# A hybrid decoder layer on one core: router fed from rows without the first norm, output projection in another order

## The chip, the core and the metric

The kernel runs on one core of a Trainium2 chip. Its time is the device time of one execution in microseconds (us); three runs are summed up by their median, and one further execution is recorded by the profiler. TensorE does the matmuls (PE in the profile), VectorE is DVE, ScalarE is ACT, GpSimd is POOL, and SyncE is SP, whose queue issues nearly all weight loads.

## What is computed

One layer for 256 tokens of width 1024: a token mixer with an output projection, a norm, a mixture of 32 experts of which each token uses four, a second norm, and a small gated sublayer with a third norm. Cut to what bears on the change:

```
y = token_mixer(x, ...)                      # ends with (g_a*y_a + g_b*y_b + g_c*y_c) @ w_out
x = layer_norm(alpha * x + y, ln1_g, ln1_b)  # the first norm: (x - mean) * rstd * g + b
logits = x @ router_w + router_b             # 256 x 32
gates, experts = softmax and indices of the 4 largest
y = sum over a token's experts of gate * (swiglu(x @ w_gu[e] + b_gu[e]) @ w_down[e] + b_down[e])
x = layer_norm(alpha * x + y, ln2_g, ln2_b)
ple = sigmoid(x @ ple_w_gate) * (p @ ple_w_proj)
x = layer_norm(alpha * x + ple, ln3_g, ln3_b)
```

## The kernel before

**Stages.** The mixer ends at 440.17 us of the span, router and first gather at 457.04 us; then come the 32 experts, one by one, and the tail. The tokens are two tiles of 128 rows (t = 0, 1), the width is two halves of 512 columns (c) or eight blocks of 128 (k).

**Order in the mixer.** Work is written as strands (Python generators) that a small loop advances in turn, and as units: a unit is a list of products and an evacuation. Every engine runs its instructions in the order in which they were recorded. The output projection is one of these series of units: `both(kp)` is the first half of both tiles with two of the eight row blocks of `w_out`, `second(t, ...)` the second half of tile t. A weight block arrives by DMA and is split into a high and a low part (`HI`, `LO`, or the buffers `RV`, `KT`, `xh`, `xl`); three products use the two. `evac` adds the residual, takes the statistics, and starts `first_norm(t)` when a tile's two halves are done. `first_norm` writes the normalised rows to `xs`, transposes them (L1186) and multiplies them with the router's weights `rw` (L1192). `router` then finds the four largest of each row and the place of each token among the 64 slots of its experts (`posm`).

**Experts.** Tokens are gathered by a matmul: `oh` is a matrix of zeros and ones that the places give, `xs` times `oh` is the gathered, transposed activations (`gat`, L1448), which ACT copies to `xe` (L1449). A group is two experts (128 slots), so one gather of eight blocks in four pieces serves two experts. Two pieces fall into each expert of the group before, between the transposes and the down projection; their PSUM buffers are two (`ms`). The up projection (`gu`, L1485) and the down projection (`dn`, L1520) multiply with `w_gu` (8.39 MB an expert) and `w_down` (4.19 MB).

**Weights.** These 12.58 MB an expert come in tiles of 2 MiB through a ring of ten buffers: four (`F0` to `F3`) are filled with expert 0's `w_gu` during the mixer, and six (`w5` to `w0`) lie in memory that the mixer uses until its end. SP issues the loads in ring order: w5 and w4 (`w_down` of expert 0, L1387), w3 to w0 (`w_gu` of expert 1, L1375), F0 and F2 (`w_down` of expert 1), F1, F3, w5, w4 (`w_gu` of expert 2), and so on. Each issue waits until its buffer's last user is done, in order, so that one that waits holds all behind it. Issues also wait for earlier transfers with which they share one of eight completion semaphores (`DMAHW0` to `DMAHW7`), which ACT's loads use too. The two rows of the first norm, `ln1_g` and `ln1_b`, are loaded to all partitions (512 KB each) by ACT in the mixer, `norm_rows`.

**Result.** An expert's rows are spread back to the tokens by another matmul and added to `Y`; the first to be added also brings in alpha times the norm's rows (`fresh` in `spread`).

## Time and profile before

| what | us |
| --- | --- |
| median of 3 runs (lowest, highest) | 1422.58 (1421.93, 1425.25) |
| the profiled execution | 1420.59 |
| its span, first to last instruction | 1418.8 |
| PE busy in it | 1343.1 (95%) |
| DVE, ACT, POOL busy | 591.8, 372.4, 247.0 |

The page has in all 481.66 MB moved, 339 GB/s over the span. Over it, the granted clock of TensorE is 0.985 of full speed. PE's busy share is high in every stage, but an engine that is busy need not be the one that ends last: rows by stretch and the waits tell that.

### The profile page before, as it was taken

The page shows a single profiled execution, that of the slowest core. Times are in us where ns is not written, and L with a number is a line of the kernel's source. Part 1 is how long each engine was busy: PE and PEld are TensorE (multiplying, and loading weights), DVE is VectorE, ACT ScalarE, POOL GpSimd, SP SyncE. Part 2 cuts the span into 40 slices and gives each one's busy share as a digit, 9 for nine tenths or more (in the row PEclk, how much of TensorE's full clock was granted, in tenths as well). Part 3 has the DMA queues.
Part 4 walks back from the last instruction along what each step waited for, and adds up shares of the span by engine and source line. Part 5 has one row for each costly group of instructions (what it writes and reads, how often), then busy time and mean ns, then how long its engine had stood idle before and what let it go on. Part 6 is the DMA issues. An engine that isn't in the chain of part 4 may idle for free. (4 is left out here: it accounts for less than half of the span.)

```text
span 1418.8 us, 19330 instructions
## 1 busy us (share of the span) xinstructions
PE 1343.1 (95%) x7720; PEld 748.0 (53%) x7721; DVE 591.8 (42%) x1245; ACT 372.4 (26%) x743; POOL 247.0 (17%) x217
## 2 busy tenths in 40 slices
PE   8999989999999999999999999999999999989987
PEld 7989967888887334334333333333333333333326
DVE  6398985865565133223222222222223222222238
ACT  6767464644551111111111110111111100111122
POOL 5554864434561000000000000000000000000000
PEclk9999999999998999999999999999999999999998
DMA  9755455345888999999999999999999999999970
GB/s 264 215 137 138 133 180 168 113 135 181 307 303 339 367 427 430 428 428 426 428 429 428 428 426 429 430 428 428 426 429 430 428 427 428 429 428 428 428 296 30
DMA packets 122133, 481.66 MB, mean 339 GB/s; under 512 B 11340, under 2 KB 69340, under 8 KB 88632
## 3 DMA queue, kind: packets, MB, share of 16 engines
q1 hardware_dynamic: 120440, 477.16, 84.4%
q0 software_dynamic: 848, 1.86, 0.4%
q10 hardware_dynamic: 752, 1.38, 0.3%
q8 instruction: 62, 1.02, 0.3%
q14 instruction: 31, 0.25, 0.0%
HBM read 478.78 MB, written 3.42 MB: 340 GB/s over the span
## 5 line engine op out<-in xcount | busy, mean ns | idle before, releaser
L1485 PE MATMUL gu<-w,xe 128*64 128x512 f32 x1168 | 262.9, 598 | 6.6 <-DMA w<-in_w_gu_dram 6.6
L1485 PE MATMUL gu<-F,xe 128*64 128x512 f32 x880 | 199.2, 596 | 4.8 <-DMA F<-in_w_gu_dram 4.8
L428 POOL TENSOR_TENSOR LO<-w,HI 128x384 fp32r<-128x384 f32 (+1 forms) x113 | 168.4, 1491 | 165.9 <-ACT HI L423 154.6
L1485 PEld LDWEIGHTS gu<-w,xe 128*64 128x64 f32 x1168 | 81.7, 137 | 164.8 <-issue 144.1
L426 DVE TENSOR_TENSOR LO<-w,HI 128x640 fp32r<-128x640 f32 (+1 forms) x113 | 117.1, 1038 | 83.5 <-ACT HI L423 81.8
L1503 DVE TENSOR_SCALAR gc<-gu 128x256 f32<-128x256 f32 x64 | 26.9, 421 | 266.9 <-PE gu L1485 266.9
L1416 POOL DMA_DIRECT2D pt<-in_p_dram x1 | 0.8, 777 | 789.2 <-DVE lc L1507 789.2
L423 ACT CAST HI<-w 128x1024 fp32r<-128x1024 f32 x113 | 118.0, 1044 | 59.2 <-PE pjt L377 36.6
L1520 PE MATMUL dn<-w,hT 128*64 128x512 f32 x560 | 130.0, 607 | 2.0 <-ACT hT L1513 2.0
L1556 DVE TENSOR_TENSOR Y<-Y,cb 128x512 f32<-128x512 f32 x124 | 79.5, 682 | 116.3 <-PE cb L1545 116.3
L367 PE MATMUL pjt<-xh,HI 128*128 128x256 f32 x424 | 124.7, 294 | 0.0
L1485 PEld LDWEIGHTS gu<-F,xe 128*64 128x64 f32 x880 | 60.2, 136 | 119.0 <-issue 104.9
L367 PE MATMUL pjt<-xh,LO 128*128 128x256 f32 x424 | 120.5, 284 | 1.3 <-DVE LO L426 1.3
L367 PE MATMUL pjt<-xl,HI 128*128 128x256 f32 x424 | 120.1, 283 | 0.0
L1520 PE MATMUL dn<-F,hT 128*64 128x512 f32 x464 | 106.0, 598 | 0.0
L1504 ACT ACTIVATE sg<-gc 128x256 f32<-128x256 f32 x64 | 26.8, 419 | 286.4 <-DVE gc L1503 286.4
L1448 PE MATMUL gat<-oh,xs 128*128 128x128 f32 x512 | 76.2, 294 | 24.7 <-DVE oh L1456 19.9
L1448 PEld LDWEIGHTS gat<-oh,xs 128*128 128x128 f32 x512 | 64.4, 197 | 44.4 <-issue 27.7
L367 PEld LDWEIGHTS pjt<-xh,HI 128*128 128x128 f32 x424 | 81.5, 192 | 1.8 <-issue 1.1
L367 PEld LDWEIGHTS pjt<-xh,LO 128*128 128x128 f32 x424 | 81.3, 192 | 2.0 <-DVE LO L426 1.9
L367 PEld LDWEIGHTS pjt<-xl,HI 128*128 128x128 f32 x424 | 81.5, 192 | 0.3
L1493 DVE TENSOR_TENSOR gt<-gwt,gt 128x256 fp32r<-128x256 f32 x32 | 13.6, 424 | 152.2 <-ACT gt L1492 152.2
(404 smaller groups left out, 1713.2 us busy)
## 6 DMA issues: line engine op xcount, KB each, us to landing
w<-in_w_gu_dram SPq DMA_DIRECT2D x73, 2048.0 KB, 29.2
F<-in_w_gu_dram SPq DMA_DIRECT2D x51, 2048.0 KB, 29.4
w<-in_w_down_dram SPq DMA_DIRECT2D x70, 1024.0 KB, 19.3
F<-in_w_down_dram SPq DMA_DIRECT2D x58, 1024.0 KB, 21.0
w<-in_w_in_dram SPq DMA_DIRECT2D x85, 512.0 KB, 3.8
F<-in_w_gu_dram SPq DMA_DIRECT2D x8, 1024.0 KB, 6.8
w<-in_w_o_lru_dram SPq DMA_DIRECT2D x8, 512.0 KB, 4.7
w<-in_w_o_swa_dram SPq DMA_DIRECT2D x8, 512.0 KB, 3.8
```

The costliest lines, as they stand in the source:

```text
L367: pe.matmul(ps, hl[l][:, k * P:(k + 1) * P], b[r][:, k], start=k == 0 and n == 0, stop=k == KD - 1 and n == 2)
L423: act.copy(hi, s)
L426: dve.tensor_sub(lo[:, 0:n], s[:, 0:n], hi[:, 0:n].bitcast(F32))
L428: pool.tensor_tensor(out=lo[:, n:], in0=s[:, n:], in1=hi[:, n:].bitcast(F32), op=ALU.subtract)
L1416: pool.dma_start(pt, a["p"][0, 0].rearrange("(t p) c -> p t c", p=P))
L1448: pe.matmul(ps[:, kk], xs[:, t, k * P:(k + 1) * P], oh[:, t], start=t == 0, stop=t == 1)
L1485: pe.matmul(gu[64 * j:64 * j + 64, b], xe[:, k], w[:, j * D + b * 512:j * D + (b + 1) * 512], start=False, stop=k == KD - 1)
L1493: dve.tensor_sub(gt[:, 1], ps, gt[:, 0].bitcast(F32))
L1503: dve.tensor_scalar(gc[:, c], guv[:, c, 0], 7.0, None, op0=ALU.min)
L1504: act.activation(sg[:, c], gc[:, c], AF.Sigmoid, scale=1.702)
L1520: pe.matmul(dn[64 * jj:64 * jj + 64], hT[:, 2 * hf + kk, j * 64:j * 64 + 64], w[:, kk, jj * 512:(jj + 1) * 512], start=hf == j == kk == 0, ...
L1556: dve.tensor_add(y, y, pss[jj])
```

## The change

Five pieces belong together. The output projection is run in another order, in which tile 0's two halves end before tile 1's first half. Its evacuation writes rows `y` before the norm to a buffer of their own, and `logits(t, c)` transposes them half by half and multiplies them with `rw`, which has been multiplied by the norm's scale; the norm's mean and its bias are made good by two constants of 32 columns (`router_weights`). `first_norm` writes only (y − mean) · rstd, by ACT; scale and bias of the norm are applied by ACT when a gathered piece leaves PSUM (`scaled_rows`), two activations for the one copy, in all groups. The first gather begins with tile 0's eight matmuls as soon as its places are known. The residual is built in `Y` during expert 0 (`residual`), with rows that ACT loads at the start of the expert stage.

```diff
+    def places(self, dve, iota, t, e):
+        dve.tensor_tensor(out=self.oh[:, t].rearrange("p (e s) -> p e s", e=GRP), in0=iota[:, :SLOTS].unsqueeze(1).to_broadcast([P, GRP, SLOTS]),
+                          in1=self.pos[:, t, e:e + GRP].unsqueeze(2).to_broadcast([P, GRP, SLOTS]), op=ALU.is_equal)
+
+    def seat(self, dve, t, ps, sel):
+        dve.scalar_tensor_tensor(self.pos[:, t], ps, 1.0, sel, ALU.add, ALU.mult)
+        dve.tensor_scalar(self.pos[:, t], self.pos[:, t], -1.0, None, op0=ALU.add)
+
+    def second(self, dve, act, pe, ps, ones, stri):
+        pe.matmul(ps[:, :NE], ones, self.sel0, start=True, stop=False)
+        pe.matmul(ps[:, :NE], stri, self.sel, start=False, stop=True)
+        pe.matmul(ps[0:1, NE:2 * NE], ones[:, 0:1], self.sel0, start=True, stop=False)
+        pe.matmul(ps[0:1, NE:2 * NE], ones[:, 0:1], self.sel, start=False, stop=True)
+        self.seat(dve, 1, ps[:, :NE], self.sel)
+        act.copy(self.counts, ps[0:1, NE:2 * NE])
...
-        pool.dma_start(rw, a["router_w"][0].rearrange("(p k) e -> p k e", k=KD))
+        pool.dma_start(rw, a["router_w"][0].rearrange("(k p) e -> p k e", p=P))
+        for i, n in enumerate(("ln1_g", "ln1_b")):
+            pool.dma_start(rt.gb[:, i], a[n].rearrange("o (p k) -> (o p) k", k=KD))
...
+
+    lc_ = mpa.tile([P, 2, NE], F32, name="lc1")
+
+    def router_weights():
+        yield from wait("late", "att3")
+        col = lambda i: pr[:, 65 + 8 * i:73 + 8 * i].unsqueeze(2).to_broadcast([P, KD, NE])
+        rb_ = m2.tile([P, T], F32, name="rwb", tag="sq").rearrange("p (k e) -> p k e", e=NE)
+        sums_ = m2.tile([P, T], F32, name="rws", tag="sq").rearrange("p (n e) -> p n e", e=NE)
+        dve.tensor_tensor(out=rb_, in0=rw, in1=col(1), op=ALU.mult)
+        dve.tensor_reduce(out=sums_[:, 1], in_=rb_.rearrange("p k e -> p e k"), axis=AX.X, op=ALU.add)
+        yield
+        dve.tensor_tensor(out=rw, in0=rw, in1=col(0), op=ALU.mult)
+        dve.tensor_reduce(out=sums_[:, 0], in_=rw.rearrange("p k e -> p e k"), axis=AX.X, op=ALU.add)
+        yield
+        ps = yield from banks.take()
+        pe.matmul(ps[:, 0:2 * NE], ones, sums_[:, 0:2].rearrange("p n e -> p (n e)"), start=True, stop=True)
+        yield
+        dve.tensor_scalar(lc_[:, 0], ps[:, 0:NE], -1.0, None, op0=ALU.mult)
+        dve.tensor_add(lc_[:, 1], ps[:, NE:2 * NE], rb)
+        banks.done(ps)
...
             yield
-        M["gb"] = big("TG", [P, 2, D])
-        for i, n in enumerate(("ln1_g", "ln1_b")):
-            act.dma_start(M["gb"][:, i], a[n].to_broadcast([P, D]))
         M["xT"] = big("MG", [P, KD, T])
...
-                xv = xs[:, t, halves[c]]
-                dve.scalar_tensor_tensor(xv, xv, 2.0 * ALPHA, out_ps[t, c], ALU.mult, ALU.add)
-                dve.bn_stats(lns[:, t, c], xv)
+                if t not in rows:
+                    rows[t] = wp.tile([P, KD * P], F32, name="y", tag="w")
+                y = rows[t][:, halves[c]]
+                dve.scalar_tensor_tensor(y, xs[:, t, halves[c]], 2.0 * ALPHA, out_ps[t, c], ALU.mult, ALU.add)
+                dve.bn_stats(lns[:, t, c], y)
                 if c == 0 and t == 0:
                     for i in range(2):
                         M["rps", i] = yield from banks.take()
                     M["wk"] = wp.tile([P, KD * P], F32, name="wk", tag="w")
                     pool.memset(M["wk"][:, 0:80], -3.0e38)
+                spawn(logits(t, c))
...
+    def logits(t, c):
+        xT = M["xT"]
+        b = yield from banks.take()
+        for k in range(4):
+            pe.transpose(b[:, k * P:(k + 1) * P], rows[t][:, (4 * c + k) * P:(4 * c + k + 1) * P], ident)
+        act.copy(xT[:, 4 * c:4 * c + 4, t * P:(t + 1) * P], b.rearrange("p (k t) -> p k t", k=4))
+        banks.done(b)
+        yield
+        for k in range(4 * c, 4 * c + 4):
+            pe.matmul(M["rps", t][:, :NE], xT[:, k, t * P:(t + 1) * P], rw[:, k], start=k == 0, stop=k == KD - 1)
+        if c:
+            events.add(f"r{t}")
+
     def first_norm(t):
 
-        xT, gb = M["xT"], M["gb"]
-        xc = wp.tile([P, KD * P], F32, name="xc", tag="w")
+        yield
+        dve.scalar_tensor_tensor(mv[:, t, 3:4], mv[:, t, 0:1], -1.0, mv[:, t, 2:3], ALU.mult, ALU.mult)
+        y = rows[t].rearrange("p (k q) -> p q k", q=KD)
         for hf in range(2):
-            c = slice(hf * 512, (hf + 1) * 512)
-            dve.scalar_tensor_tensor(xc[:, c], xs[:, t, c], mv[:, t, 0:1], gb[:, 0, c], ALU.subtract, ALU.mult)
-        qk = lambda v, hf: v.rearrange("p (k q) -> p q k", q=KD)[:, 4 * hf:4 * hf + 4]
-        for hf in range(2):
-            dve.scalar_tensor_tensor(xs[:, t, 512 * hf:512 * hf + 512].rearrange("p (q k) -> p q k", q=4), qk(xc, hf),
-                                     mv[:, t, 2:3], qk(gb[:, 1], hf), ALU.mult, ALU.add)
-        if t == 0:
-            yield
-        else:
-            events.add("n1")
-        for hf in range(2):
-            b = yield from banks.take()
-            for k in range(4):
-                pe.transpose(b[:, k * P:(k + 1) * P], xs[:, t, (4 * hf + k) * P:(4 * hf + k + 1) * P], ident)
-            act.copy(xT[:, 4 * hf:4 * hf + 4, t * P:(t + 1) * P], b.rearrange("p (k t) -> p k t", k=4))
-            banks.done(b)
-        if t == 0:
-            yield
-        for k in range(KD):
-            pe.matmul(M["rps", t][:, :NE], xT[:, k, t * P:(t + 1) * P], rw[:, k], start=k == 0, stop=k == KD - 1)
-        events.add(f"r{t}")
+            act.activation(xs[:, t, 512 * hf:512 * hf + 512].rearrange("p (q k) -> p q k", q=4), y[:, 4 * hf:4 * hf + 4],
+                           AF.Identity, scale=mv[:, t, 2:3], bias=mv[:, t, 3:4])
+        events.add(f"n{t}")
...
-        yield from wait("r0", "n1")
+        yield from wait("r0", "n0")
...
         for t in range(2):
             if t:
-                yield from wait("r1")
-            dve.tensor_add(lg[:, t, :NE], M["rps", t][:, :NE], rb)
+                yield from wait("r1", "n1")
+            dve.scalar_tensor_tensor(lg[:, t, :NE], lc_[:, 0], mv[:, t, 0:1], M["rps", t][:, :NE], ALU.mult, ALU.add)
+            dve.scalar_tensor_tensor(lg[:, t, :NE], lg[:, t, :NE], mv[:, t, 2:3], lc_[:, 1], ALU.mult, ALU.add)
...
-            ps2 = yield from banks.take()
             if t == 0:
+                rt.softmax(dve, 0, ex[0], sel[0], sm[0][:, 1:2])
+                yield
+                ps2 = yield from banks.take()
                 pe.matmul(ps2[:, :NE], stri, sel[0], start=True, stop=True)
-                rt.softmax(dve, 0, ex[0], sel[0], sm[0][:, 1:2])
-            else:
-                pe.matmul(ps2[:, :NE], ones, sel[0], start=True, stop=False)
-                pe.matmul(ps2[:, :NE], stri, sel[1], start=False, stop=True)
-                pe.matmul(ps2[0:1, NE:2 * NE], ones[:, 0:1], sel[0], start=True, stop=False)
-                pe.matmul(ps2[0:1, NE:2 * NE], ones[:, 0:1], sel[1], start=False, stop=True)
-                act.copy(rt.counts, ps2[0:1, NE:2 * NE])
-            dve.scalar_tensor_tensor(posm[:, t], ps2[:, :NE], 1.0, sel[t], ALU.add, ALU.mult)
-            dve.tensor_scalar(posm[:, t], posm[:, t], -1.0, None, op0=ALU.add)
-            banks.done(ps2)
+                yield
+                rt.seat(dve, 0, ps2[:, :NE], sel[0])
+                banks.done(ps2)
+                rt.places(dve, iota, 0, 0)
...
-    for work, done in ((both(0), ()), (both(1), ()), (second(0, 0, 1), ()), (both(2), ()), (both(3), ((0, 0), (1, 0))),
-                       (second(0, 2, 3), ((0, 1),)), (second(1, 0, 1), ()), (second(1, 2, 3), ((1, 1),))):
+    first = lambda t, *kps: [(t, 0, kp) for kp in kps]
+    for work, done in ((both(0), ()), (both(1), ()), (second(0, 0, 1), ()), (first(0, 2, 3), ((0, 0),)),
+                       (second(0, 2, 3), ((0, 1),)), (first(1, 2, 3), ((1, 0),)), (second(1, 0, 1), ()), (second(1, 2), ()),
+                       (second(1, 3), ((1, 1),))):
         units.append(out_unit(work, done))
...
-    def gathered(oh, n, xe, first=False):
+    def scaled_rows(xe, k2, ps):
+        for kk in range(2):
+            k = 2 * k2 + kk
+            act.activation(xe[:, k], ps[:, kk], AF.Identity, scale=rt.gb[:, 0, k:k + 1], bias=rt.gb[:, 1, k:k + 1])
+
+    def gathered(oh, n, xe):
         for k2 in range(KD // 2):
-            if first:
-                ps = p1.tile([P, 2, n], F32, name="gat", tag="cb", bufs=3)
-            else:
-                ps = p1.tile([P, 2, n], F32, name="gat", tag="ms")
+            ps = p1.tile([P, 2, n], F32, name="gat", tag="ms")
             for kk in range(2):
                 k = 2 * k2 + kk
                 for t in range(2):
                     pe.matmul(ps[:, kk], xs[:, t, k * P:(k + 1) * P], oh[:, t], start=t == 0, stop=t == 1)
-            act.copy(xe[:, 2 * k2:2 * k2 + 2], ps)
+            scaled_rows(xe, k2, ps)
             yield
 
     def group(e):
-        oh = w2.tile([P, 2, GRP, SLOTS], F32, name="oh1", tag="oh1", bufs=1)
-        for t in range(2):
-            dve.tensor_tensor(out=oh[:, t], in0=iota[:, :SLOTS].unsqueeze(1).to_broadcast([P, GRP, SLOTS]),
-                              in1=posm[:, t, e:e + GRP].unsqueeze(2).to_broadcast([P, GRP, SLOTS]), op=ALU.is_equal)
         xe = w2.tile([P, KD, GRP * SLOTS], F32, name="xe", tag="xe")
         ahead.append(xe)
-        yield
-        yield from gathered(oh.rearrange("p t e s -> p t (e s)"), GRP * SLOTS, xe, e == 0)
+        if e:
+            for t in range(2):
+                rt.places(dve, iota, t, e)
+            yield
+            yield from gathered(rt.oh, GRP * SLOTS, xe)
+            return
+
+        pss = [p1.tile([P, 2, GRP * SLOTS], F32, name="gat", tag="cb", bufs=3) for _ in range(3)]
+        pss.append(p1.tile([P, 2, GRP * SLOTS], F32, name="gat", tag="ms"))
+        for t in range(2):
+            if t:
+                rt.second(dve, act, pe, p1.tile([P, 2 * NE], F32, name="seats", tag="tr"), ones, stri)
+                rt.places(dve, iota, 1, 0)
+            for k in range(KD):
+                pe.matmul(pss[k // 2][:, k % 2], xs[:, t, k * P:(k + 1) * P], rt.oh[:, t], start=t == k % 2 == 0, stop=t == k % 2 == 1)
+                if t and k % 2:
+                    scaled_rows(xe, k // 2, pss[k // 2])
+                    yield
+
+    def residual():
+        g1, b1 = (w2.tile([P, D], F32, name=n, tag=n, bufs=1) for n in ("ob", "bd"))
+        for v, n in ((g1, "ln1_g"), (b1, "ln1_b")):
+            act.dma_start(v, a[n].to_broadcast([P, D]))
+        yield
+        qk = lambda v: v.rearrange("p (k q) -> p q k", q=KD)
+        for t in range(2):
+            for hf in range(2):
+                q = slice(4 * hf, 4 * hf + 4)
+                dve.scalar_tensor_tensor(qk(Y[:, t])[:, q], xs[:, t].rearrange("p (q k) -> p q k", q=KD)[:, q],
+                                         ALPHA, qk(g1)[:, q], ALU.mult, ALU.mult)
+            for hf in range(2):
+                c = halves[hf]
+                dve.scalar_tensor_tensor(Y[:, t, c], b1[:, c], ALPHA, Y[:, t, c], ALU.mult, ALU.add)
+            yield
+        got.append(w2.tile([NE, D], F32, name="bd", tag="bd", bufs=1))
+        pool.dma_start(got[0], a["b_down"][0])
...
-                if t in fresh:
...
-                else:
-                    dve.tensor_add(y, y, pss[jj])
+                dve.tensor_add(y, y, pss[jj])
                 then(t, jj)
...
     gu, first = begun(0), gather
-    next(first)
-    rt.finish(dve)
+    rest = residual()
+    next(rest)
     for _ in range(2):
         next(first)
+    rt.finish(dve)
     for e in range(NE):
         if e % GRP == 0:
...
         def mid(k):
             if e == 0:
                 next(first, None)
+                if k in (3, 5, 7):
+                    next(rest, None)
```

How instructions move is seen in the order of SP first. These are the loads between the two stages: w5 and w4 down projection of expert 0, w3 to w0 up projection of expert 1, F0 the first refill. Before:

```order
L1387 DMA w5_4808<-in_w_down_dram 128x2048 [waits DMASW2_49,DMASW1_49,DMASW0_49]
L1387 DMA w5_4808<-in_w_down_dram 128x2048
L1387 DMA w4_4823<-in_w_down_dram 128x2048 [waits DMAHW3_49,DMASW5_49,PE_49]
L1387 DMA w4_4823<-in_w_down_dram 128x2048 [waits DMAHW4_49]
L1375 DMA w3_4846<-in_w_gu_dram 128x4096 [waits DVE_49,DMAHW5_49,PE_49,Pool_49]
L1375 DMA w2_4856<-in_w_gu_dram 128x4096 [waits DVE_49,DMAHW6_49,PE_49,Pool_49]
L1375 DMA w1_4871<-in_w_gu_dram 128x4096 [waits DMAHW7_49,Activation_49]
L1375 DMA w0_4881<-in_w_gu_dram 128x4096 [waits DMAHW0_49]
```

Of the change:

```order
L1430 DMA w5_4836<-in_w_down_dram 128x2048 [waits DMASW3_49,DMASW4_49,DMASW1_49,DMASW5_49,DMASW0_49,PE_49]
L1430 DMA w5_4836<-in_w_down_dram 128x2048
L1430 DMA w4_4851<-in_w_down_dram 128x2048 [waits DVE_49,DMAHW3_49,PE_49,Pool_49]
L1430 DMA w4_4851<-in_w_down_dram 128x2048 [waits DMAHW4_49]
L1418 DMA w3_4874<-in_w_gu_dram 128x4096 [waits DMAHW5_49,Activation_49]
L1418 DMA w2_4884<-in_w_gu_dram 128x4096 [waits DVE_49,DMAHW6_49,PE_49,Pool_49]
L1418 DMA w1_4899<-in_w_gu_dram 128x4096 [waits DMAHW7_49,DVE_49]
L1418 DMA w0_4909<-in_w_gu_dram 128x4096 [waits DMAHW0_49]
```

The order of the loads stays; the wait for the engines that split and use `LO` (DVE, PE and POOL together) moves from w3 to w4, since the memory plan of the mixer has moved, and w1 waits for DVE (the instruction L1257, which reads a constant that lies in w1's memory) where it waited for ACT.

PE, from the last output products to the first up projection (`gu`), before:

```order
L377 MATMUL pjt<-KT,AT 128x512
L1186 MATMUL pg<-cst,xs 128x128 x8
...
L1186 MATMUL pg<-cst,xs 128x128 x8
L1192 MATMUL pg<-rw,MG 128x32 x8
L1223 MATMUL pg<-wk,cst 128x32
L1226 MATMUL pg<-wk,ones 128x32
L1227 MATMUL pg<-tail,cst 128x32
L1228 MATMUL pg<-wk,ones 1x32
L1229 MATMUL pg<-tail,ones 1x32
L1448 MATMUL gat<-oh_4697,xs 128x128 x8
L1485 MATMUL gu<-F_97,xe 64x512 x4
L1448 MATMUL gat<-oh_4697,xs 128x128 x4
```

Of the change:

```order
L403 MATMUL pjt<-KT,AT 128x512
L1269 MATMUL pg<-tail,cst 128x32
L1220 MATMUL pg<-cst,y 128x128 x4
...
L1225 MATMUL pg<-rw,MG 128x32 x4
L1515 MATMUL gat<-oh_71,xs 128x128 x8
L120 MATMUL seats<-tail,ones 128x32
L121 MATMUL seats<-tail,cst 128x32
L122 MATMUL seats<-tail,ones 1x32
L123 MATMUL seats<-tail,ones 1x32
L1515 MATMUL gat<-oh_71,xs 128x128 x4
L1561 MATMUL gu<-F_99,xe 64x512 x4
L1515 MATMUL gat<-oh_71,xs 128x128 x2
```

Three groups of four transposes and three router groups have moved ahead of the last output product, four of each stand behind it; eight gather matmuls (tile 0) stand ahead of the places of tile 1 (`seats`), and four instead of eight between these and the first up projection.

## Rows read from the trace of the kernel before

**Rows 1.** Windows: engines' busy us (instructions), PEclk, DMA share, GB/s.
```profile
550.00:1050.00 500.00, 485.89 (x2416) 192.15 (x2414) 133.43 (x306) 60.80 (x151) 0.00 (x0) 1.00 1.01 428
...
420.00:460.00 40.00, 37.40 (x189) 30.21 (x187) 23.35 (x61) 7.99 (x14) 7.71 (x9) 0.87 0.87 355
420.00:500.00 80.00, 74.61 (x364) 44.81 (x364) 28.93 (x76) 13.47 (x26) 7.71 (x9) 0.91 0.88 358
460.00:464.00 4.00, 4.00 (x23) 1.93 (x24) 0.00 (x0) 0.74 (x2) 0.00 (x0) 1.00 0.22 51
```

**Rows 2.** PE's waits, 1040 to 1305: us in all, times, longest.
```profile
PE gu L1485 <- DMA w<-in_w_gu_dram: 6.6, 8, 1.4
```

**Rows 3.** Timeline of ACT: the last CAST of experts 1, 3, 23, 29.
```profile
515.30 0.58 ACT L1533 CAST ob<-dn 128x512 fp32r<-128x512 f32 x1 [4.17 <-PE dn L1520]
...
570.19 0.58 ACT L1533 CAST ob<-dn 128x512 fp32r<-128x512 f32 x1 [4.17 <-PE dn L1520]
...
1134.06 0.58 ACT L1533 CAST ob<-dn 128x512 fp32r<-128x512 f32 x1 [4.17 <-PE dn L1520]
...
1313.28 0.58 ACT L1533 CAST ob<-dn 128x512 fp32r<-128x512 f32 x1 [4.17 <-PE dn L1520]
```

**Rows 4.** Timeline of SP: DMAs it issues between the stages.
```profile
418.57 1.85 SPq L1387 DMA_DIRECT2D w<-in_w_down_dram  x4
432.25 0.33 SPq L1375 DMA_DIRECT2D w<-in_w_gu_dram  x1
440.41 1.28 SPq L1375 DMA_DIRECT2D w<-in_w_gu_dram  x3
461.98 6.00 SPq L1387 DMA_DIRECT2D F<-in_w_down_dram  x4
```

**Rows 5.** Timeline of PE: transposes, router, gathers, first up projection.
```profile
440.17 1.14 PE L1186 MATMUL pg<-cst,xs 128*128 128x128 f32 x8
...
442.92 1.08 PE L1192 MATMUL pg<-rw,MG 128*128 128x32 f32 x8
...
453.20 3.91 PE L1448 MATMUL gat<-oh,xs 128*128 128x128 f32 x16 [0.35 <-DVE oh L1456]
457.04 1.94 PE L1485 MATMUL gu<-F,xe 128*64 128x512 f32 x8
```

**Rows 6.** Timeline of DVE: residual sum, places of tile 1.
```profile
440.43 0.70 DVE L1153 SCALAR_TENSOR_TENSOR xs<-xs,pjt 128x512 f32<-128x512 f32 x1
...
453.10 0.19 DVE L1231 SCALAR_TENSOR_TENSOR GP<-pg,tail 128x32 f32<-128x32 f32 x1
...
453.54 0.29 DVE L1456 TENSOR_TENSOR oh<-cst,GP 128x128 f32<-128x128 f32 x1
```

**Rows 7.** Groups of ACT by shape, whole run, columns as on the page.
```profile
L1449 ACT COPY xe<-gat 128x256 f32<-128x256 f32 x64 | 23.8, 372 | 79.3 <-PE gat L1448 79.3
...
L460 ACT ACTIVATE AT<-pjt,pr 128x256 f32<-128x256 f32 x8 | 4.5, 562 | 5.5 <-PE pjt L367 5.5
```

**Rows 8.** Timeline of ACT and PE in expert 2.
```profile
533.20 0.37 ACT L1449 COPY xe<-gat 128x256 f32<-128x256 f32 x1 [2.38 <-PE gat L1448]
533.49 0.37 ACT L1513 COPY hT<-tr 128x256 f32<-128x256 f32 x1
533.62 1.05 PE L1448 MATMUL gat<-oh,xs 128*128 128x128 f32 x7 [0.23 <-ACT xe L1449]
```

**Rows 9.** Timeline of DVE: first norm, first operation of expert 0.
```profile
438.21 2.32 DVE L1177 SCALAR_TENSOR_TENSOR xs<-xc,mv,TG 128x512 f32<-128x512 f32 x2
...
474.04 0.42 DVE L1503 TENSOR_SCALAR gc<-gu 128x256 f32<-128x256 f32 x1 [7.92 <-PE gu L1485]
```

**Rows 10.** Timeline of POOL: the router's load, a split.
```profile
26.30 0.59 POOL L220 DMA_DIRECT2D rw<-in_router_w_dram  x1
...
31.46 1.02 POOL L428 TENSOR_TENSOR LO<-w,HI 128x384 fp32r<-128x384 f32 x1 [1.97 <-ACT HI L423]
```

More of the change, by code (lines that the diff above doesn't have):

```diff
@@ L26 @@
 SLOTS = 64
+GRP = 2
 NR = T // SLOTS - 1
@@ L93, in __init__ @@
         self.pick = pl.tile([96, 32], BF16, name="pick")
-        tail = pl.tile([P, 100], F32, name="tail")
+        tail = pl.tile([P, 132], F32, name="tail")
+        self.oh = pl.tile([P, 2, GRP * SLOTS], F32, name="oh1")
+        self.sel0 = tail[:, 100:100 + NE]
+        self.gb = pl.tile([P, 2, KD], F32, name="gb1")
         self.ex, self.sel, self.sm, self.counts = tail[:, 0:NE], tail[:, NE:2 * NE], tail[:, 64:66], tail[0:1, 68:68 + NE]
@@ L1329, in moe @@
     sync, act, dve, pool, pe = nc.sync, nc.scalar, nc.vector, nc.gpsimd, nc.tensor
-    ident, iota = (cst[:, i * P:(i + 1) * P] for i in (0, 2))
+    ident, stri, iota = (cst[:, i * P:(i + 1) * P] for i in range(3))
     G, posm = rt.G, rt.pos
@@ L1395, in moe @@
     Y = me.tile([P, 2, D], F32, name="Y")
-    bd = w2.tile([NE, D], F32, name="bd", tag="bd", bufs=1)
-    pool.dma_start(bd, a["b_down"][0])
+    got = []
     def down_biases():
@@ L1408, in down_biases @@
                 ps = p1.tile([P, 512], F32, name="cb", tag="cb", bufs=3)
-                pe.matmul(ps, gT[:, t * P:(t + 1) * P], bd[:, hf * 512:(hf + 1) * 512], start=True, stop=True)
+                pe.matmul(ps, gT[:, t * P:(t + 1) * P], got[0][:, hf * 512:(hf + 1) * 512], start=True, stop=True)
                 sl = slice(hf * 512, (hf + 1) * 512)
```

22 lines of the change are left out of this document (8 added, 14 removed).

## The prediction

> **What bounds the kernel now.** I read the busy time in windows first, then the waits of PE, then the stretch around the change on each engine. Between 550 and 1050 us the transfers fill the 16 DMA engines (share 1.01, 428 GB/s) while PE is busy too [rows 1]; the two run side by side, and the question is which one ends last. PE's waits answer it [rows 2]: in the last 265 us before 1305 it waits eight times for weights of an up projection; the like query of 470 to 1040 lists no DMA at all. So PE falls behind or is level at first and has caught up with the transfers by about 1060 us. From there the stream of weights sets the time, up to the last of those waits near 1300, behind which PE needs the same work as now. **The end moves as the stream moves**, unless PE uses up its slack.
>
> That slack can be read. The last CAST of experts 1 and 3 is at 515.30 and 570.19: two experts take 54.89 us when PE does not wait. From expert 23 (1134.06) to expert 29 (1313.28) six of them take 179.22 us [rows 3]. 179.22 − 3 × 54.89 = 14.6 us: PE could lose that much before it, and not the stream, set the end. It is a floor, since earlier waits of the 1040 to 1305 stretch lie outside it.
>
> **Where the stream stands.** SP issues weights in a fixed order, and the new order of the output projection changes what SP waits for. Before: both halves of w5 and of w4 at 418.57, w3 at 432.25, three at 440.41, F0 at 461.98 [rows 4]. w3 was released by the last product that read LO, w2 by the last that read KT, 36 products later: 8.16 / 36 = 0.227 us a product. In the changed order w4's memory is the one that waits for LO, and behind that product come 24 products, 8 transposes and 12 router matmuls.
>
> The last output product ended with the transposes' start, at 440.17 [rows 5]. In front of it now stand three groups of four transposes (8 take 1.14, so 1.7) and three router groups (1.08 each: a group of 4 is 8 records, so 3.2), and one 128x32 matmul (0.3): it ends near 445.4. Back from there by 24 × 0.227 + 1.1 + 3.2 = 9.8: w4 is released near 435.6 instead of 418.6, w3 right behind it, w2 at 445.5. Between 460 and 464 the mean is 51 GB/s, 0.2 MB, half a microsecond at full rate: first bytes come 1.5 us after an issue. So the stream holds w5 and the rest of the output weights at first and is idle to about 437.3, some 11 us in which it moved data before.
>
> What does it lose? Before, it moved 14.2 MB from 420 to 460 (355 GB/s) and 28.66 MB to 500 (358) [rows 1]: six tiles of 2.097 MB and the norm's two rows (1.05 MB) are 13.63, so 0.57 MB were the end of the output weights. It was idle too, from before 458 to 463.5, since F0 waited for the first products of expert 0 with all else landed. In the changed kernel w4 lands later, but the gap closes: w5 and the rest (2.67 MB) until the pause, then 62.7 us from 437.3 to 500 at 428.5 GB/s, 26.87 MB; less 0.13 MB for b_down, which moves into this stretch, 0.75 MB more than before. **0.75 MB at 428.5 GB/s: −1.75 us.**
>
> Against that, short holes. w1 waits for the vector instruction of tile 1's logits, which reads the memory under it, near 450.5 (below), 452 with latency, when w2 has just landed: 0.4. w0 shares a completion semaphore with ln1_g, now issued by ACT behind tile 1's exponential (~452) and not in the mixer; it can't be issued before ln1_g has landed. If that row (0.52 MB) goes behind w2 and w1 it lands near 459.5, and w0's bytes start at 461 instead of 460: 1 to 2.2 us of hole; if the rows share the engines with the stream, none. F0 needs expert 0's products (459.5 to 462.5), by which time the stream has w0 to move. Together 0 to 3.5; I take **+0.7**. The Trainium skill ("DMA: Bandwidth & Descriptors", section "Queues, rings and completion order") states that each DMA engine goes round the queue rows that have work, a packet at a time, so ACT's row would not queue behind SP's tiles; by that rule this hole is 0 and the sum 0.7 lower. No row of before shows two such queues loaded at once.
>
> **PE's own start.** Tile 1's last half: result into y 0.70 [rows 6], 4 transposes 0.6, a copy 0.6, router group 1.08: logits near 449.5. Then 8 gather matmuls of tile 0, which used to run with tile 1's; at full clock (16 passes at half clock took 3.91 [rows 5], 7 passes at full clock 1.05 [rows 8]) 1.2, at half clock 2.3. The places of tile 1 (0.19 to 0.29 each on DVE, 0.73 in all [rows 6]) and four gathers follow: the first up projection begins at 455.0 to 457.6, 457.04 before. I take 455.0 and 1.2 us less of gathers behind it: PE gains 3.2 us, and the slack is 14.6 + 3.2 = 17.8. It is worth nothing at the end as long as the stream leads.
>
> **The evacuation of gathered rows.** One 128x256 copy (372 ns, 64 of them) becomes two 128x128 activations with a scale and a bias per partition; a 128x256 one takes 562 [rows 7]. A 128x512 CAST is 580 ns [rows 3] against 372 at 256 columns, so 128 columns are 0.104: one is 562 − 104 = 0.458. The copy behind a 0.37 us copy starts 0.29 after it [rows 8], so they overlap by 0.08: a pair is 0.836, +0.46. Bounds: two copies of 128 columns (2 × 0.268, +0.16) and two activations at the price of a 128x256 one (2 × 0.562, +0.76). PE waits for it: gathers have two buffers, and expert 2's gather waits 0.23 for ACT [rows 8]; two per expert may add the rest, 30 in fifteen groups, 30 × 0.46 = 13.8 us, at the upper bound 22.8. **13.8 is under 17.8: hidden by the stream.** Only what lies behind the last DMA wait shows, the gather for experts 30 and 31: **+0.46**. The Trainium skill ("ScalarE: Activation LUTs", section "What ACT_TABLE_LOAD costs") gives 186 ns + 0.833 ns a column, 93 ns for each pointer operand and 93 ns of overlap: an estimate of 865 ns for the pair, +0.49, 30 of them 14.7, still hidden; rows 7 agree with it (399 against 372, 585 against 562).
>
> **What is hidden elsewhere.** The first norm leaves DVE (four of these, two take 2.32 [rows 9], off the path to the gather) and becomes two activations of tile rows on ACT, idle then. The residual, eight DVE operations (4 × 1.16 + 4 × 0.70 = 7.4), goes into expert 0, where DVE idles 7.92 before 474.04 [rows 9]; uncovered it would cost that 7.4 once on PE, inside the slack. The router's weights cost four DVE operations and one 128x64 matmul (0.3, counted with the stream's start). On POOL two tiny loads (0.59 each, a piece of the 26.30 row) precede splits that idle 1.97 [rows 10]; uncovered, 1.2 us on the mixer.
>
> **Sum.** 1420.59 (the profiled execution: span 1418.8 and 1.8 around it) − 1.75 + 0.7 + 0.46 = 1420.0. The median of the runs is 1.99 above the profiled one: **1422.0**.
>
> **Rivals.**
> 1. *PE's gain reaches the end.* If PE and not the stream sets the end, the earlier start counts: at most 2.0 + 1.2, with a faster clock over the stretch 4.3; 1422.58 − 4.3 = 1418.3. Against it: the eight waits of rows 2. Chance 0.12.
> 2. *ACT becomes the bound (slower).* If a pair costs 0.76 more, 30 of them are 22.8, 5.0 above the slack of 17.8, and the last adds 0.76: 1422.58 + 5.8 = 1428.3. It decides from 0.59 us a pair on (17.8 / 30). For it: PE waits for this copy already. Against it: the 0.46 worked out. Chance 0.14.
> 3. *SP stands at w0 for ln1_g.* The rows land behind the stream at half the rate or later, hole 3.1 and not 0.7: 1422.0 + 2.4 = 1424.4. Chance 0.12.
>
> **How the numbers follow.** The forecast has 0.62, its own range 1420 to 1425 from the holes (0 to 3.5) and the evacuation's bounds. What a measurement tells from no change is 0.3%, 4.3 us. Faster by more: half of rival 1 and a bit of the forecast, 0.08; slower: rival 2 and the tail of rival 3, 0.16; the rest, 0.76, is no change. The range, 1418.3 to 1428.3, runs from rival 1's time to rival 2's.
>
> **What would show it.** SP's issues: w5 at 418.6 and the next at 435.6, w2 near 445.5, w0 behind ln1_g's landing; no DMA idle from 440 to 500 but the holes; first up projection at 455 to 457.6; 64 pairs of 0.84; PE waiting for xe in every group by 0.4 to 0.5 more, and still for weights behind 1060, by about 15 us less in all over the run. If PE waits for no weights near the end, rival 2 holds; if gaps near 458 to 462 remain, rival 3. Wrong would be the forecast if pairs cost 0.6 more, or if the late w4 (needed for expert 0's down projection, near 480) makes PE wait.

## The result, and the profile after

The change is slower: 1430.8 us median (1425.13 to 1434.74, 20 runs) against 1421.65 (1416.9 to 1425.25, 20 runs); the ratio is 1.0061, 95% interval 1.0049 to 1.0072. The forecast was 1422.0, no change, with 1428.3 as its upper end. The profiled execution of the change has a span of 1429.2 us (1418.8 before).

First the stage of the experts, windows of the changed kernel with the columns of [rows 1]:

```profile
550.00:1050.00 500.00, 478.30 (x2351) 188.40 (x2350) 129.65 (x298) 72.65 (x181) 0.00 (x0) 0.99 1.01 425
420.00:460.00 40.00, 38.22 (x216) 31.01 (x217) 21.50 (x62) 16.42 (x24) 9.03 (x11) 1.00 0.72 283
420.00:500.00 80.00, 74.96 (x392) 44.53 (x393) 33.72 (x85) 23.52 (x39) 9.59 (x12) 1.00 0.85 339
460.00:464.00 4.00, 4.00 (x20) 1.29 (x16) 0.00 (x0) 1.51 (x4) 0.00 (x0) 1.00 0.94 345
```

The DMA engines are as busy as before (1.01) and move 425 GB/s where they moved 428. Nothing in the forecast provided for that: it used 428.5 throughout. What it costs from 550 us to the last loads near 1370 can be estimated: 820 × 3 / 425 = 5.8 us by the rounded rates, and 5.1 us by 427.9 and 425.3, the rates that the bytes of the traced packets give.

Second, SP's loads between the stages, from its timeline:

```profile
415.94 7.76 SPq L442 DMA_DIRECT2D w<-in_w_out_dram  x4
423.92 17.47 SPq L1430 DMA_DIRECT2D w<-in_w_down_dram  x4
441.49 24.11 SPq L1418 DMA_DIRECT2D w<-in_w_gu_dram  x4
466.56 1.91 SPq L1430 DMA_DIRECT2D F<-in_w_down_dram  x4
```

The pattern is the forecast one (w5, then a long wait until w4 is released, both within the 17.47 us; then w3 to w0, the last behind a second long wait), but its first load stands 5.35 us later than in [rows 4]: the mixer is late. Here are DVE's timeline of the kernel before (first row, the seventh of its splits into `LO`) and that of the change (second row the same split, third row what follows it), and POOL's of the change:

```profile
26.26 0.82 DVE L426 TENSOR_TENSOR LO<-w,HI 128x640 fp32r<-128x640 f32 x1
29.27 0.94 DVE L452 TENSOR_TENSOR LO<-w,HI 128x640 fp32r<-128x640 f32 x1
30.14 4.79 DVE L317 SCALAR_TENSOR_TENSOR spe<-spe,spq 128x8 f32<-128x8 f32 x2
29.47 0.97 POOL L244 DMA_DIRECT2D rw<-in_router_w_dram  x1
```

The split is 3.0 us late already. Then two instructions on 8 columns take 4.79 us together, to 34.93, while POOL issues the router's load (0.97, in 1024 pieces) and the two small ones, from 29.47 to 31.53.

Third, PE's start and what it waits for. PE's timeline from the first gather to the first up projection, then three of its waits of 1040 to 1305, then the last CAST of experts 1, 3, 23 and 29 on ACT's:

```profile
452.53 2.03 PE L1515 MATMUL gat<-oh,xs 128*128 128x128 f32 x16
...
456.05 1.13 PE L1515 MATMUL gat<-oh,xs 128*128 128x128 f32 x8 [0.92 <-DVE tail L104]
457.28 1.94 PE L1561 MATMUL gu<-F,xe 128*64 128x512 f32 x8
```

```profile
PE gat L1493 <- ACT xe L1485: 5.4, 9, 0.7
PE gu L1561 <- DMA F<-in_w_gu_dram: 2.7, 3, 1.3
PE gu L1561 <- DMA w<-in_w_gu_dram: 1.9, 4, 0.8
```

```profile
514.12 0.58 ACT L1609 CAST ob<-dn 128x512 fp32r<-128x512 f32 x1 [4.17 <-PE dn L1596]
...
571.42 0.58 ACT L1609 CAST ob<-dn 128x512 fp32r<-128x512 f32 x1 [4.17 <-PE dn L1596]
...
1148.57 0.58 ACT L1609 CAST ob<-dn 128x512 fp32r<-128x512 f32 x1 [4.17 <-PE dn L1596]
...
1325.67 0.58 ACT L1609 CAST ob<-dn 128x512 fp32r<-128x512 f32 x1 [4.17 <-PE dn L1596]
```

Against [rows 3] PE is 1.2 us early at expert 1 in spite of the late mixer, 14.5 late at expert 23 and 12.4 at expert 29. From 1040 to 1305 it still waits for weights seven times, 4.6 us: the stream still ends last, as in [rows 2], but it is later.

### The profile page after: what moved, and what is told of

Same layout as the page of the kernel before. It is cut to its first block, busy times and chain, and to the rows that moved or that the text cites. A ratio compares the mean times of both kernels' runs of the same rounds, so it can differ in the third digit from the quotient of the medians.

```text
span 1429.2 us, 19387 instructions
## 1 busy us (share of the span) xinstructions
PE 1340.4 (94%) x7722; PEld 745.5 (52%) x7723; DVE 593.1 (41%) x1255; ACT 402.9 (28%) x811; POOL 248.6 (17%) x219
## 5 line engine op out<-in xcount | busy, mean ns | idle before, releaser
L1493 PE MATMUL gat<-oh,xs 128*128 128x128 f32 x480 | 71.2, 293 | 37.8 <-DVE oh L110 20.0
L1493 PEld LDWEIGHTS gat<-oh,xs 128*128 128x128 f32 x480 | 59.9, 196 | 55.5 <-issue 26.5
L1596 PEld LDWEIGHTS dn<-w,hT 128*64 128x64 f32 x560 | 37.8, 140 | 73.1 <-issue 62.6
```

Of the source, the lines that this page charges most:

```text
L1493: pe.matmul(ps[:, kk], xs[:, t, k * P:(k + 1) * P], oh[:, t], start=t == 0, stop=t == 1)
L1596: pe.matmul(dn[64 * jj:64 * jj + 64], hT[:, 2 * hf + kk, j * 64:j * 64 + 64], w[:, kk, jj * 512:(jj + 1) * 512], start=hf == j == kk == 0, ...
```

## The experiments

What the 1216 bytes of new tiles (`oh1`, `gb1`, a larger `tail`) do is seen in the memory plan of the two kernels, here the address within a partition of the first early buffer and the first late one, and their offsets within 256 and 512:

```
          F0      mod 256  mod 512     w0      mod 256  mod 512
before    20480      0        0       129440     160      416
change    21696    192      192       129632      96       96
```

Three theories were set against each other. **R**: the place of the buffers slows the stream. **P**: POOL's loads hold up DVE and so the mixer. **E** (rival 2 of the prediction): ACT's pairs make PE the bound.

**The router's loads on ACT** (`e1_rw_on_act`):

```diff
-        pool.dma_start(rw, a["router_w"][0].rearrange("(k p) e -> p k e", p=P))
+        act.dma_start(rw, a["router_w"][0].rearrange("(k p) e -> p k e", p=P))
         for i, n in enumerate(("ln1_g", "ln1_b")):
-            pool.dma_start(rt.gb[:, i], a[n].rearrange("o (p k) -> (o p) k", k=KD))
+            act.dma_start(rt.gb[:, i], a[n].rearrange("o (p k) -> (o p) k", k=KD))
```

> The changed kernel, with the router's weights (1024 pieces of 128 bytes) and the two small rows of the norm issued by ACT instead of POOL, nothing else. Theory P (POOL's load): in the changed kernel a vector instruction on 8 columns that starts beside POOL's three loads ends 4 us late and the mixer never makes it up; expects that this instruction takes 0.2 to 0.5 us again, the first w_down load issued by SP near 420 instead of 423.9, and a median 4 us below the changed kernel's 1430.8, near 1427. Theory J (the early lateness is the jitter of the first transfers): the first w_down load stays near 424 and the time within 2 us of 1430.8. Theory E (the pairs of activations on ACT hold PE and so set the end): an earlier mixer gives back all of what it gains only where PE leads at the end, also about 4 us, but the waits of PE for weights near the end are gone.

1427.45 us (five runs, 1425.88 to 1429.01), 3.4 under the change; ratio to before 1.0047 (1.0033 to 1.0061). The two instructions take 1.66 us instead of 4.79, and the first w_down load goes at 418.54:

```profile
29.96 1.66 DVE L317 SCALAR_TENSOR_TENSOR spe<-spe,spq 128x8 f32<-128x8 f32 x2
418.54 17.52 SPq L1430 DMA_DIRECT2D w<-in_w_down_dram  x4
```

P holds here, for a third of the loss.

**The change with the buffers' offsets of before** (`e2_aligned`):

```diff
-        tail = pl.tile([P, 132], F32, name="tail")
+        tail = pl.tile([P, 212], F32, name="tail")
```

> The changed kernel with 320 bytes a partition of unused memory behind the router's tile, so that each of the ten weight buffers begins at the same offset within 512 bytes as in the kernel before (0 for F0 to F3, 416 for w0 to w5, where the change has 192 and 96). Theory R (place): the weights stream at 425 GB/s instead of 428 since the change moved the buffers; expects 428 GB/s between 550 and 1050 us and a median some 5 us lower, near 1426. Theory X (the rate differs from execution to execution, whatever the kernel): no change of the median beyond 1.5 us, and a rate of 425 or 428 by chance. Theory E (ACT's pairs): rate and median unchanged.

1421.22 us, ratio 0.9997 (0.9986 to 1.0009): all of the loss is gone, the part of POOL's loads too, though they are still there. Its windows (the last row is the kernel before, for comparison), SP's loads (the second row is the last two of the first row's four, w4's), two rows of PE, CASTs of experts 1, 23 and 29, and PE's longest waits from 470 to 1400:

```profile
550.00:1050.00 500.00, 477.72 (x2338) 189.94 (x2336) 130.85 (x300) 74.18 (x185) 0.00 (x0) 0.98 1.01 428
420.00:460.00 40.00, 38.22 (x217) 28.15 (x217) 17.38 (x58) 16.00 (x26) 6.26 (x8) 1.00 0.73 296
426.00:436.00 10.00, 10.00 (x53) 8.44 (x52) 5.84 (x10) 2.14 (x4) 2.41 (x5) 1.00 0.04 8
456.00:462.00 6.00, 6.00 (x30) 2.24 (x32) 2.75 (x4) 2.46 (x4) 0.00 (x0) 1.00 0.77 269
420.00:600.00 180.00, 170.08 (x863) 81.07 (x863) 58.12 (x146) 35.79 (x75) 6.82 (x9) 0.98 0.94 395
420.00:600.00 180.00, 171.48 (x854) 83.84 (x854) 59.59 (x143) 25.65 (x57) 7.71 (x9) 0.96 0.95 397
```

```profile
418.03 17.51 SPq L1430 DMA_DIRECT2D w<-in_w_down_dram  x4
...
434.73 0.80 SPq L1430 DMA_DIRECT2D w<-in_w_down_dram  x2
435.64 24.08 SPq L1418 DMA_DIRECT2D w<-in_w_gu_dram  x4
460.67 1.85 SPq L1430 DMA_DIRECT2D F<-in_w_down_dram  x4
```

```profile
446.70 2.03 PE L1515 MATMUL gat<-oh,xs 128*128 128x128 f32 x16
451.45 1.94 PE L1561 MATMUL gu<-F,xe 128*64 128x512 f32 x8
```

```profile
509.83 0.58 ACT L1609 CAST ob<-dn 128x512 fp32r<-128x512 f32 x1 [4.17 <-PE dn L1596]
...
1145.81 0.58 ACT L1609 CAST ob<-dn 128x512 fp32r<-128x512 f32 x1 [4.17 <-PE dn L1596]
...
1315.29 0.58 ACT L1609 CAST ob<-dn 128x512 fp32r<-128x512 f32 x1 [4.17 <-PE dn L1596]
```

```profile
PE gat L1493 <- ACT xe L1485: 17.9, 30, 0.7
PE gat L1493 <- DVE oh L110: 17.8, 14, 1.6
```

This is nearly the kernel that the prediction described: w4's release at 434.73 (435.6 forecast), 30 waits for ACT, PE 5.5 us early at expert 1, 11.8 late at expert 23, and 2.0 late at expert 29, where the kernel before has been waiting for the stream. One thing differs. Among the waits from 470 to 1400 there is none for weights, where the kernel before has thirteen, 11.4 us: here PE comes too late to wait for the stream. (The waits for `oh` are those of before, 19.6 us there.)

**The reverse**: before with the change's loads (`e3_before_pieces`), and before with the change's places (`e4_before_shifted`).

```diff
         pool.dma_start(rw, a["router_w"][0].rearrange("(p k) e -> p k e", k=KD))
+        rw2 = mp.tile([P, KD, NE], F32, name="rw2")
+        pool.dma_start(rw2, a["router_w"][0].rearrange("(k p) e -> p k e", p=P))
+        gb2 = mp.tile([P, 2, KD], F32, name="gb2")
+        for i, n in enumerate(("ln1_g", "ln1_b")):
+            pool.dma_start(gb2[:, i], a[n].rearrange("o (p k) -> (o p) k", k=KD))
```

> The kernel before, with three more loads by POOL behind its load of the router's weights, into memory that nothing reads: the same weights in 1024 pieces of 128 bytes and the two rows of the norm in pieces of 32 bytes. Theory P: a vector instruction beside them ends 4 us late, the mixer ends about 4 us later (first w_down load near 422.5), and the median is 4 us higher, near 1425.7. Theory J: within 1 us of the kernel before.

```diff
-        tail = pl.tile([P, 100], F32, name="tail")
+        tail = pl.tile([P, 404], F32, name="tail")
```

> The kernel before with 1216 bytes a partition of unused memory behind the router's tile, so that the ten weight buffers stand at the changed kernel's offsets within 512 bytes (192 for F0 to F3, 96 for w0 to w5). Theory R: 425 GB/s instead of 428 between 550 and 1050, and a median some 5 us higher, near 1427. Theory X and theory E: the median stays within 1.5 us of the kernel before.

The loads alone: 1421.39, ratio 0.9998 (0.9989 to 1.0008), nothing. The places alone: 1426.33, ratio 1.0033 (1.0021 to 1.0045), +4.9 us, and in its windows 425 GB/s:

```profile
550.00:1050.00 500.00, 483.64 (x2400) 190.64 (x2398) 132.60 (x303) 60.53 (x151) 0.00 (x0) 1.00 1.01 425
```

R holds, in both directions. P as it was put fails: the loads cost nothing where the buffers stand as before.

**Which buffers, and whether P or the pairs count there.** `e5` moves only what lies early in memory (F0 to F3, the mixer's tiles and Y), `e6` only w0 to w5, each by unused memory; `e7` is `e1` and `e2` in one; `e8` shares the evacuation out.

```diff
     def scaled_rows(xe, k2, ps):
-        for kk in range(2):
-            k = 2 * k2 + kk
-            act.activation(xe[:, k], ps[:, kk], AF.Identity, scale=rt.gb[:, 0, k:k + 1], bias=rt.gb[:, 1, k:k + 1])
+        k = 2 * k2
+        act.activation(xe[:, k], ps[:, 0], AF.Identity, scale=rt.gb[:, 0, k:k + 1], bias=rt.gb[:, 1, k:k + 1])
+        dve.tensor_scalar(xe[:, k + 1], ps[:, 1], rt.gb[:, 0, k + 1:k + 2], rt.gb[:, 1, k + 1:k + 2], op0=ALU.mult, op1=ALU.add)
```

> The kernel before with unused memory placed so that F0 to F3 (and the mixer's tiles) stand 192 bytes off a multiple of 512, as in the changed kernel, while w0 to w5 keep their offset of 416. Theory R (place) in the form that F counts: 425 to 426 GB/s between 550 and 1050 us, median 3 to 5 us above the kernel before. In the form that only w counts: 428 and no change. If every buffer pays for itself, four of ten, 427 and +2 us.

> The kernel before with 192 bytes of unused memory ahead of w0 only: F0 to F3 keep offset 0 within 512, w0 to w5 go from 416 to 96 as in the changed kernel. Theory R in the form that w counts: 425 to 426 GB/s and +3 to +5 us; in the form that only F counts: 428 and no change; if every buffer pays for itself, six of ten, 426.5 and +3 us.

> The changed kernel with the buffers at the offsets of before (as in e2_aligned) and the router's three loads issued by ACT (as in e1_rw_on_act). Theory P, that POOL's loads in pieces hold up the vector engine and so the mixer whatever the place of the buffers: 3 to 4 us below e2_aligned, near 1418. Theory P2, that they do so only where the mixer is already late in its first 30 us, as with the moved buffers: within 1 us of e2_aligned's 1421.2.

> The changed kernel with the buffers at the offsets of before, and each gathered piece evacuated by ACT (first half) and DVE (second half) side by side instead of twice by ACT. Both theories expect PE's waits for xe to fall from 17.9 us to 9 or less. Theory S (the stream of weights ends last, PE's slack hides the pairs): the median stays within 1.5 us of e2_aligned's 1421.2, and PE waits for weights again near the end. Theory E (the pairs set the end): 4 to 8 us lower, near 1415.

`e5`: 1427.34, ratio 1.0042 (1.0027 to 1.0057), 425 GB/s. `e6`: 1421.0, 0.9995 (0.9985 to 1.0004), 428 GB/s. So the early buffers decide and the late ones, as they were moved here, don't. `e7`: 1422.42, 1.0003 (0.9994 to 1.0012): with the offsets of before the loads on POOL cost nothing (P2). `e8`: 1422.8, 1.0004 (0.9991 to 1.0017). The waits for `xe` did not fall but rose to 20.7 us, so this run does not test the pairs: ACT and DVE wrote halves of one tile and went one after the other, DVE (second row) beginning when ACT (first row) is done:

```profile
530.14 0.46 ACT L1484 ACTIVATE xe<-gat,gb 128x128 f32<-128x128 f32 x1 [2.39 <-PE gat L1493]
530.64 0.41 DVE L1485 TENSOR_SCALAR xe<-gat,gb 128x128 f32<-128x128 f32 x1 [1.61 <-ACT xe L1484]
```

**The pairs taken away** (`e9_aligned_copy`; the scale and bias of the gathered rows are left out), and three more places.

```diff
     def scaled_rows(xe, k2, ps):
-        for kk in range(2):
-            k = 2 * k2 + kk
-            act.activation(xe[:, k], ps[:, kk], AF.Identity, scale=rt.gb[:, 0, k:k + 1], bias=rt.gb[:, 1, k:k + 1])
+        act.copy(xe[:, 2 * k2:2 * k2 + 2], ps)
```

> The changed kernel with the buffers at the offsets of before, and the gathered pieces copied out of PSUM by one ACT copy of 256 columns, as the kernel before does; the norm's scale and bias of the gathered rows are left out (the router's are not, so the same tokens go to the same experts). Both theories expect PE's waits for xe to fall from 17.9 us to about 3.4. Theory S (the stream ends last and hides the pairs): the median is 0 to 1.5 us below e2_aligned's 1421.2, and PE waits for weights by 10 us or more near the end, as in the kernel before. Theory E (the pairs set the end): 5 to 10 us lower, near 1413.

> The kernel before with 192 bytes of unused memory between F0 to F3 and the tiles of the expert stage: F0 to F3 and the mixer's tiles stay where they are, Y and what follows moves by 192 bytes, w0 to w5 keep their offset of 416 within 512. Theory R in the form that F (or a tile of the mixer) counts: 428 GB/s, the median within 1 us of the kernel before, and no lateness in the first 35 us. In the form that Y counts (all of the slow kernels have moved it too): 425 and +5 us.

> The kernel before with F0 to F3 and the mixer's tiles moved by 256 bytes (offset 256 within 512), w0 to w5 at 416 as before. Theory R512 (512 bytes is what counts for these tiles): 425 GB/s and +5 us, as with 192. Theory R256 (a smaller unit counts, which 192 misses and 256 meets): 428 and no change.

> The changed kernel with F0 to F3 and also w0 to w5 at offset 0 within 512 (416 in the kernel before and in e2_aligned). If the offset of w0 to w5 counts at all, the packets into w0, w1, w2 and w4, which take 310 to 311 ns in the median where those into F0 take 309, come down too, 429 to 430 GB/s, and 2 to 4 us are gained on e2_aligned's 1421.2. If it doesn't, as e6_before_late_shifted says, the median is within 1 us of it.

`e9`: 1421.25, 0.9994 (0.9985 to 1.0003), as `e2`. PE's waits from 470 to 1400 are of the kind of the kernel before again, for weights 17.7 us in all:

```profile
PE gu L1559 <- DMA w<-in_w_gu_dram: 9.1, 10, 1.3
PE gu L1559 <- DMA F<-in_w_gu_dram: 8.6, 9, 1.2
PE gat L1491 <- ACT xe L1483: 3.4, 15, 0.2
```

E falls: 14.5 us of waits for ACT are exchanged for waits for weights, at no gain clear of noise. `e10` (Y moved): 1422.23, 0.9999 (0.9991 to 1.0008). With Y ruled out, and since the mixer's tiles are out of use by 550 us, F0 to F3 are what is left for the 425 GB/s there. `e11` (early tiles by 256 bytes): 1421.0, 0.9996 (0.998 to 1.0012), 428 GB/s. `e12` (all ten at offset 0): 429 GB/s, but 1421.06, 0.9992 (0.9982 to 1.0002).

**The unit, and the change once more.** `e13` and `e14` move the early tiles by 128 and 64 bytes, `e15` the late ones by 32.

> The kernel before with F0 to F3 and the mixer's tiles moved by 128 bytes, w0 to w5 at offset 416 within 512. If multiples of 128 are enough for F: 428 GB/s between 550 and 1050 us and no change. If 256 are needed: 425 and +5 us.

> The kernel before with F0 to F3 and the mixer's tiles moved by 64 bytes, w0 to w5 at 416. If every offset that is no multiple of 128 (or 256) is slow: 425 GB/s and +5 us, as with 192. If 192 alone is slow: no change.

> The kernel before with w0 to w5 moved by 32 bytes, to offset 448 within 512 (192 within 256, where F is slow); F0 to F3 unmoved. If the offset counts for any buffer that the weights go to: 425 GB/s and +3 to +5 us. If only F0 to F3 or the mixer's tiles count: no change.

> The changed kernel once more, for a second trace. Theory P2 (moved tiles make the first 30 us late, POOL's three loads fall on a vector instruction then, and both together pass what the mixer can make up): the vector instruction on 8 columns behind 30 us takes about 4 us again, the first w_down load is issued near 423 to 424, time near 1430. Theory J (an accident of the one execution that was traced): the load is issued near 419 and the time is near 1426.

| kernel before with | offset mod 256: F0 to F3 | w0 to w5 | GB/s, 550 to 1050 | ratio (interval) |
| --- | --- | --- | --- | --- |
| nothing | 0 | 160 | 428 | 1 |
| e11 | 0 (256 further) | 160 | 428 | 0.9996 (0.998, 1.0012) |
| e14 | 64 | 160 | 425 | 1.0034 (1.0022, 1.0046) |
| e13 | 128 | 160 | 425 | 1.0030 (1.0017, 1.0042) |
| e5 | 192 | 160 | 425 | 1.0042 (1.0027, 1.0057) |
| e6 | 0 | 96 | 428 | 0.9995 (0.9985, 1.0004) |
| e15 | 0 | 192 | 428 | 0.9999 (0.9990, 1.0008) |
| e17 | 0 | 0 | 429 | 0.9977 (0.9965, 0.9989) |

The change again (`e16`): 1425.88, 1432.07 and 1433.64 us. The traced one is the first of these. Its two instructions on DVE take 3.12 us this time, and the mixer has made that up before its end:

```profile
29.08 3.12 DVE L317 SCALAR_TENSOR_TENSOR spe<-spe,spq 128x8 f32<-128x8 f32 x2
```

```profile
418.94 0.81 SPq L1430 DMA_DIRECT2D w<-in_w_down_dram  x2
```

So neither P2 nor J as put: the stall recurs, but this execution makes it up (1425.88, what the places alone would cost), where the first traced one stayed late by 5 us. How many of the untraced ones stayed late is not known.

**What all buffers at offset 0 are worth** (`e17`: the kernel before with 96 unused bytes ahead of w0; `e18`: `e9` with the same).

```diff
     Y = me.tile([P, 2, D], F32, name="Y")
+    me.tile([P, 24], F32, name="unused")
```

> The kernel before with w0 to w5 moved by 96 bytes to offset 0 within 512, F0 to F3 unmoved at 0. Theory S2 (the stream ends last here, and in the changed kernel with all buffers at 0 it is PE that does): 429 GB/s and some 2 to 4 us less than the kernel before, 1418 to 1420. If the offset of w0 to w5 only changes the packets' times and not the end: within 1 us of the kernel before.

> The changed kernel with F0 to F3 and w0 to w5 all at offset 0 within 512, and the gathered pieces copied by one ACT copy (the norm's scale and bias of the gathered rows are left out, as in e9_aligned_copy). Theory S2 (PE with the pairs is the bound in e12_aligned_all): 1417 to 1419, as the kernel before with all buffers at 0. If the pairs cost nothing there either: near e12_aligned_all's 1421.

`e17`: 1418.14, 0.9977 (0.9965 to 0.9989), faster than both kernels. `e18`: 1418.69, 0.9982 (0.9971 to 0.9993). `e12`, with the pairs, stays at 0.9992 (0.9982 to 1.0002); PE's waits of 1040 to 1305 in it:

```profile
PE gat L1494 <- ACT xe L1486: 5.9, 10, 0.7
PE gu L1562 <- DMA F<-in_w_gu_dram: 1.2, 1, 1.2
```

One wait for weights is left where `e17` has eleven (9.7 us): with the faster stream PE ends last, and there the pairs begin to cost. The intervals of `e12` and `e18` overlap, so this last point is supported, not settled.

## Why the prediction was wrong

**The step that failed** is one that was not written down: the sum took 428.5 GB/s from the kernel before for the changed one, and counted only what the change does in time, not what it does in memory. Its new tiles are allocated ahead of F0 and moved the early buffers from offset 0 to 192 within 256. That costs 4.9 us alone (`e4`), and 9.6 us in the changed kernel (1430.8 against `e2`'s 1421.22).

**The rest of that, some 3 to 5 us, is POOL's loads** (3.4 by `e1`, 4.7 as what is left), which the prediction priced at "1.2 us on the mixer" if uncovered. Two things were missed: what they hold up is not POOL's next split but an instruction on DVE beside them, and 1024 pieces are not the load of before. With the offsets of before the stall is short and made up (`e2`, `e3`; without the loads, in `e7`, the time is no better). With moved buffers the mixer is already 1.4 to 1.9 us late at 17 us (DVE's fourth split), in each of the seven traces of this kind, and the two add. Four traces show it at the load that SP issues at 49.79 in the kernel before: it goes at 50.13 in `e4` (places alone), 50.45 in `e1` and 50.76 in `e16`, nearly made up, but at 54.43 in the change's first trace. The times agree: the 25 runs of `e4`, `e5`, `e13` and `e14` have a median of 1426.55 (1422.91 to 1430.6), the 23 of the change one of 1430.84 (1425.13 to 1434.74).

**Right in part**, by `e2`, in which only the places differ: the time is that of before, 1421.22 (forecast 1422.0), and w4, the pairs and the slack came out near their sizes. That the sum fits so well is partly luck, since the stream's gain and holes together came out with the other sign, and since PE, which was to stay hidden, uses up all of its slack. Term by term:

- *w4's late release and the pause*: forecast 435.6 for w4, w3 right behind it, and idle to 437.3; w4 at 434.73, w3 at 435.64, and 8 GB/s from 426 to 436.
- *The stream's gain of 1.75 and its holes of 0.7*: the holes were mis-sized. Over 420 to 600 us `e2` moves 395 GB/s and the kernel before 397, 0.36 MB or 0.8 us less, where 1.05 more was forecast: holes of some 2.6 us and not 0.7, near the 3.1 of rival 3. The four loads of w3 to w0 take 24.08 us to issue: SP stands at w0 for ln1_g until 459.4, as rival 3 has it, and the rate from 456 to 462 is 269 GB/s. The packets of `e2`'s trace, summed by microsecond of their start and by the queue that issued them, show why:

```
us (start)             452   453   454   455   456   457   458   459   460
SP's tiles, MB        0.38  0.26  0.34  0.31  0.26  0.03  0     0     0.26
ACT's two rows, MB    0.02  0.10  0.07  0.06  0.07  0.26  0.39  0.07  0
```

  The rows move beside the tiles, but at a quarter of the bytes from 453 to 457, since their packets are small (4 KB, against 16 KB). They are through only when the tiles are, and by then SP has nothing else issued. The Trainium skill ("DMA: Bandwidth & Descriptors", section "Queues, rings and completion order") says that queue rows take turns by packet, and the trace agrees: from 453 to 457 us 73 packets of ACT's rows start and 72 of SP's tiles. The prediction's conclusion from it, a hole of 0, which its sum did not use, was wrong, since turns by packet are no equal shares of bytes.
- *PE's start*: forecast 455.0 (457.04 before); in `e2` the first up projection begins at 451.45. The last output product ends at 443.7 (445.4 forecast) and the router's last group at 446.9 (449.5 forecast), with the clock granted in full (1.00 from 420 to 460; 0.87 before, with 0.50 from 448 to 456). One term was too small: tile 0's eight gather matmuls are 16 passes and took 2.03 us where 1.2 was forecast, 3.91 at half clock in [rows 5]. At expert 1 PE leads by 5.5 us.
- *The pair*: forecast 0.836 from 0.458 each; 128 activations take 453 ns on average and a pair 0.81. 30 waits, 17.9 us against 3.4, 14.5 more; 13.8 was forecast from [rows 7, 8].
- *Slack*: 17.8 forecast. In `e2` PE has used it up: 2.0 late at expert 29, and no wait for weights from 470 to 1400, where the prediction had PE "still" waiting for them behind 1060. So in `e2` the end no longer follows the stream; the two are level. It hid the pairs, with nothing to spare: `e9`, without them, waits for weights again and has the same median.
- *A misreading*: the prediction counts eight waits for weights near the end, but [rows 2] shows one of two rows. With those for F0 to F3 (4.8 us, five times) it is thirteen waits and 11.4 us, so "about 15 us less" could not be.

Of the rivals, 2 did not happen in the changed kernel, which still waits for weights; in `e2` its sign is there (PE waits for none), but not its price of 5.8 us (`e9`). That 1428.3 was not far from the time is the right size with the wrong cause. Rival 1's start was there and bought nothing. Rival 3's hole was there too and did not show in the time of `e2`.
